# A trunk of Fourier and attention layers: the exact front scales its tables, and the even outputs are added to x outside PSUM

## The chip, the cores and the metric

The kernel runs on one core of one Trainium2 chip. The metric is the device time of one execution in microseconds (us), given as the median of several runs. Five engines matter: TensorE (in profiles PE, with its weight loads as PEld), VectorE (DVE), ScalarE (ACT), GpSimd (POOL) and SyncE (SP). SP, ACT and POOL also issue transfers (DMA), each into its own queue. A transfer issued by POOL can add what it moves to what stands at its destination; such a transfer is called an adding transfer below.

## The reference

Two sequences, `x_prompt` and `x_sample`, each of 512 tokens by 1024 features in float32, pass through the same trunk of two layers. Each layer is a token mixer and an MLP, both behind an RMS norm and both added to x. The mixer of layer 0 is a grouped 2-D Fourier transform, that of layer 1 is attention.

```
def fourier_mix(h, w_out):
    hg = h.reshape(B, S, N_FGROUPS, F_GROUP)          # 8 groups of 128 features
    f = jnp.fft.fft2(hg, axes=(1, 3), norm="ortho").real
    return f.reshape(B, S, D_MODEL) @ w_out

def sq_relu_mlp(h, w_up, w_down):
    a = jnp.maximum(h @ w_up, 0)
    return (a * a) @ w_down

for i in range(2):
    x = x + (fourier_mix if i == 0 else gqa_attention)(rms_norm(x, ...), ...)
    x = x + sq_relu_mlp(rms_norm(x, mlp_norm[i]), mlp_w_up[i], mlp_w_down[i])
return rms_norm(x, final_norm)
```

The change lies in the first 70 us or so, in the Fourier mixer of layer 0 for both sequences. Sequence 0 is `x_prompt`, sequence 1 is `x_sample`.

## The kernel before, in words

**Order.** The whole kernel is written inside `manual_schedule`: each engine executes its instructions in the order in which the program names them, and so do the three queues that issue transfers. A line in the Python text therefore has a place in each engine's list. Waits between engines follow from the data. PSUM has eight banks, handed out by `ps()` in turn, and most tiles in SBUF come from one ring of equal slots, handed out by `slot()`.

**The transform.** The tokens are folded so that a transform of 512 tokens needs two products, a cosine one ("even") and a sine one ("odd"), of half the length; the features of a group are folded in the same way, so that a feature transform is again an even and an odd product. `Front` (L394) prepares a pair of token tiles of 128 tokens: `squares` sums the squares of a tile on ScalarE, `chain` makes the reciprocal root of the norm from them in six small steps (L146 is one of them), `gain` (L410) multiplies by the gains, `plus` and `minus` (L423) fold the features, `plus_there` (L419) does the first of these by an adding transfer inside SBUF, `scale` and `scale_both` (L434, L440) apply the root on ScalarE, and `combine` (L441) folds two token tiles into one by VectorE (L449 for sequence 0, L464 and L465 for sequence 1). For sequence 0 the tiles 0 and 1 aren't folded with each other, so there are three chunks of the token sum in `parts`: tile 0, tile 1, and tiles 2 and 3 together.

**Exact and split products.** Sequence 0 goes first and uses full float32 in its transform, where a product is a pair of matmuls (`exact_even` L504, `exact_odd` L507, and `exact_nyq` L510 for the eight features that the fold leaves over). Its tables come from `exact_table`. Sequence 1, and all products with weights, split each operand into a high and a low half in a faster format, the high half cast by ScalarE (L86) and the low one subtracted by VectorE (L87), and take three matmuls (`mm3`, L81 to L83).

**`transform(q, mid, hook)`** (L578) makes the token products of chunk 0 and 1, calls `mid`, makes those of the last chunk, takes each pair from PSUM (`seq_evac`) and makes four feature stages (`feat_stage`, L541), the results of which go to `uv`. L553 is a product that picks the sums of the odd features, four times per sequence; L552 and L544 are the feature products, L596 and L597 take the left-over rows out of PSUM as `an`. `hook` is called after every stage and puts other work there. Before it, `idle` (L576) issues 39 products of a constant tile, whose result nobody reads.

**The weights** of the mixer come in four pairs, `Fold(0)` to `Fold(3)` (L636): `minus` subtracts on VectorE (L645) and sends an adding transfer of 512 KB from DRAM (L646); `odd` splits the differences, `even_hi` and `even_lo` split the sums (L655, L659). `FoldNyq` does it for the rows left over (L677, L679).

**The outputs.** `odd_outs(0, ...)` makes the odd half of all eight output blocks of sequence 0 in eight PSUM banks. `odd_put` (L720, L721) copies them to x, twice: once as they are and once with the sign turned. `even_outs` then makes the even half, block by block: 12 matmuls of `mm3` and one for the rows left over (L697). `even_put` adds it to both halves of x by VectorE from PSUM (L726), and ScalarE copies the two edge columns (L727). After every second block, `add_input` (L730) sends an adding transfer of 512 KB that brings in the input itself; x is kept as four pairs of blocks, `xs[0, 0]` to `xs[0, 3]`, of 512 KB each. Between these calls stand the steps of the front of sequence 1 (`g0`, `g1`) and the four tables of its transform (`table(k)`, L329, issued by POOL).

**What follows.** SP puts away one pair of sequence 0, loads x of sequence 1 and the first MLP weights. `transform(1)` runs with `hook1`: after its first three token stages ScalarE squares the blocks 0, 1 and 2 of x of sequence 0, after its feature stages the blocks 3 to 7 (`square`, L178), and POOL adds the squares up (L182). Then `even_outs(1)` and `odd_outs(1)` follow, with the MLP of sequence 0 behind them.

## Time and profile before

| | before |
|---|---|
| median of 3 runs | 1672.26 us (1671.59 to 1673.68) |
| the profiled execution | 1673.12 us |
| its span, first to last instruction | 1671.3 us |
| mean granted TensorE clock | 0.999 |
| TensorE busy | 1661.9 us (99%) |
| VectorE busy | 1267.0 us (76%) |
| ScalarE busy | 872.1 us (52%) |
| GpSimd busy | 394.3 us (24%) |
| moved by transfers | 302.48 MB, mean 181 GB/s |

A row of the timeline gives the start of an instruction in us from the span's start, its busy time, the engine, the line of the kernel and the operation, then what it writes and reads by the program's names, and in brackets the idle time of the engine just before it with what ended that. A row ending in x6 stands for six such instructions in sequence. A row of the view of windows gives a stretch, its length, the busy time and number of instructions of each engine (PE, PEld, DVE, ACT, POOL in that order), the granted clock, the busy share of the transfer engines and what they moved in GB/s. In the list of transfers a row ends with the number, the size and the median time from issue to landing.

### The profile page before, as it was taken

The page shows a single profiled execution, that of the slowest core. Times are in us where ns is not written, and L with a number is a line of the kernel's source. Part 1 is how long each engine was busy: PE and PEld are TensorE (multiplying, and loading weights), DVE is VectorE, ACT ScalarE, POOL GpSimd, SP SyncE. Part 2 cuts the span into 40 slices and gives each one's busy share as a digit, 9 for nine tenths or more (in the row PEclk, how much of TensorE's full clock was granted, in tenths as well). Part 3 has the DMA queues.
Part 4 walks back from the last instruction along what each step waited for, and adds up shares of the span by engine and source line. Part 5 has one row for each costly group of instructions (what it writes and reads, how often), then busy time and mean ns, then how long its engine had stood idle before and what let it go on. Part 6 is the DMA issues. An engine that isn't in the chain of part 4 may idle for free.

```text
span 1671.3 us, 22288 instructions
## 1 busy us (share of the span) xinstructions
PE 1661.9 (99%) x7843; PEld 1387.8 (83%) x7843; DVE 1267.0 (76%) x1851; ACT 872.1 (52%) x1540; POOL 394.3 (24%) x364
## 2 busy tenths in 40 slices
PE   9999999999999999999999999999999999999998
PEld 8988887888888888888888888888888888888887
DVE  8879776557886869869888877777855487878875
ACT  7766444446342435447688855554454552433334
POOL 3321444221000001325444303004422220000002
PEclk9999999999999999999999999999999999999999
DMA  9843554449775757425501156334544696757532
GB/s 306 257 158 118 204 195 172 151 170 373 250 228 165 248 170 236 168 77 200 166 1 39 64 176 223 117 120 167 211 145 166 221 375 194 233 158 236 178 104 101
DMA packets 122192, 302.48 MB, mean 181 GB/s; under 512 B 12344, under 2 KB 13496, under 8 KB 122080
## 3 DMA queue, kind: packets, MB, share of 16 engines
q1 hardware_dynamic: 98720, 253.53, 43.9%
q0 software_dynamic: 8960, 21.05, 6.0%
q10 hardware_dynamic: 14400, 26.48, 4.2%
q8 instruction: 61, 1.00, 0.2%
q14 instruction: 51, 0.42, 0.1%
HBM read 217.59 MB, written 82.38 MB: 179 GB/s over the span
## 4 chain that ended last, share of the span: by engine, by line
PE 97%; DVE 1%; DMA 0%; ACT 0%; issue 0%; POOL 0%; DVEq 0%; POOLq 0%; ACTq 0%
PE ps L940 74%; PE ps L83 6%; PE ps L81 6%; PE ps L82 6%; PE ps L1535 2%; PE ps L576 0%; PE ps L1514 0%; DMA raw<-w_up 0%; PE ps L191 0%; PE ps L507 0%; PE ps L504 0%; DVE w L87 0%; DVE raw L990 0%; PE ps L199 0%; DVE raw L989 0%
## 5 line engine op out<-in xcount | busy, mean ns | idle before, releaser
L940 PE MATMUL ps<-u,w 128*128 128x512 f32 x4944 | 1130.9, 389 | 1.2 <-DVE t L1018 1.2
L940 PEld LDWEIGHTS ps<-u,w 128*128 128x128 f32 x4944 | 926.6, 188 | 195.9 <-ACT u L973 1.7
L86 ACT CAST w<-raw 128x1024 fp32r<-128x1024 f32 (+1 forms) x216 | 213.7, 994 | 311.5 <-PE ps L940 234.3
L87 DVE TENSOR_TENSOR w<-raw,w 128x1024 fp32r<-128x1024 f32 (+1 forms) x216 | 252.0, 1170 | 75.7 <-ACT w L86 75.4
L86 ACT CAST u<-u 128x1024 fp32r<-128x1024 f32 x144 | 145.0, 1047 | 85.1 <-PE ps L940 36.4
L87 DVE TENSOR_TENSOR u<-u,u 128x1024 fp32r<-128x1024 f32 x144 | 174.3, 1239 | 17.3 <-ACT u L86 16.0
L940 PE MATMUL ps<-u,u 128*128 128x512 f32 x600 | 143.3, 389 | 0.0
L1150 DVE TENSOR_TENSOR u<-ps,u 128x512 f32<-128x512 f32 x160 | 109.9, 688 | 39.8 <-PE ps L940 37.3
L1177 POOL DMA_DIRECT2D raw<-w_sum x32 | 27.7, 865 | 468.2 <-DMA raw<-w_sum 170.8
L1058 POOL TENSOR_TENSOR u<-u 128x512 f32<-128x512 f32 x28 | 37.0, 1321 | 425.9 <-ACT u L955 425.9
L940 PEld LDWEIGHTS ps<-u,u 128*128 128x128 f32 x600 | 112.5, 188 | 24.1 <-ACT u L973 0.4
L81 PE MATMUL ps<-u,u 128*128 128x512 f32 (+2 forms) x340 | 128.7, 380 | 0.0
L83 PE MATMUL ps<-u,u 128*128 128x512 f32 (+2 forms) x340 | 123.7, 365 | 0.0
L82 PE MATMUL ps<-u,u 128*128 128x512 f32 (+2 forms) x340 | 123.6, 365 | 0.0
L182 POOL TENSOR_TENSOR t<-t,t 128x512 f32<-128x512 f32 (+1 forms) x54 | 79.2, 1470 | 187.0 <-ACT t L178 186.1
L954 ACT ACTIVATE t<-t 128x512 f32<-128x512 f32 x64 | 40.5, 632 | 109.2 <-DVE t L1027 95.7
L83 PEld LDWEIGHTS ps<-u,u 128*128 128x128 f32 x340 | 64.2, 189 | 10.5 <-DVE u L87 0.3
L87 DVE TENSOR_TENSOR u<-ps,u 128x512 fp32r<-128x512 f32 (+3 forms) x112 | 68.2, 636 | 5.6 <-ACT u L86 5.0
L82 PEld LDWEIGHTS ps<-u,u 128*128 128x128 f32 x340 | 64.4, 189 | 8.5 <-DVE u L87 0.3
L81 PEld LDWEIGHTS ps<-u,u 128*128 128x128 f32 x340 | 64.4, 189 | 7.8
L1014 DVE TENSOR_TENSOR t<-ps,u 128x512 f32<-128x512 f32 x32 | 22.0, 689 | 59.5 <-PE ps L940 55.8
L86 ACT CAST u<-ps 128x512 fp32r<-128x512 f32 (+3 forms) x112 | 59.5, 557 | 7.7 <-PE ps L1535 6.1
(270 smaller groups left out, 2024.6 us busy)
## 6 DMA issues: line engine op xcount, KB each, us to landing
raw<-w_up SPq DMA_DIRECT2D x80, 512.0 KB, 4.6
u<-spill_t SPq DMA_DIRECT2D x60, 512.0 KB, 6.7
raw<-w_sum SPq DMA_DIRECT2D x56, 512.0 KB, 5.5
u<-spill_b SPq DMA_DIRECT2D x45, 512.0 KB, 6.3
spill_t<-u SPq DMA_DIRECT2D x84, 256.0 KB, 2.0
spill_b<-t ACTq DMA_DIRECT2D x60, 256.0 KB, 4.4
raw<-w_row SPq DMA_DIRECT2D x28, 512.0 KB, 5.0
park<-u SPq DMA_DIRECT2D x24, 512.0 KB, 4.6
```

Source lines behind the costliest of these rows:

```text
L81: nc.tensor.matmul(out, lh, rh, start=first, stop=False)
L82: nc.tensor.matmul(out, lh, rl, start=False, stop=False)
L83: nc.tensor.matmul(out, ll, rh, start=False, stop=last)
L86: hi = nc.scalar.copy(dst_hi, src)
L87: return hi, eng.tensor_sub(dst_lo, src, f32(dst_hi))
L182: nc.gpsimd.tensor_add(acc[q][:, :n], acc[q][:, :n], s[:, :n])
L940: nc.tensor.matmul(o, w[x][:, sl], h[k][y], start=first and k + i == 0, stop=k == n - 1 and i == 2, skip_group_check=not first)
L954: nc.scalar.activation(t, src, AF.Relu)
L1058: eng.tensor_sub(t[:, 0], b12, b11)
L1150: return nc.vector.tensor_add(x, o, x)
L1177: nc.gpsimd.dma_start(s[:, 1], w[:, 3], accum_op=ALU.add)
L1535: nc.tensor.transpose(pt[:, t * P : (t + 1) * P], probs[t][:, sc * P : (sc + 1) * P], ident)
```

## The change

**The front of sequence 0.** The root of the norm is no longer applied to the folded operands of tiles 0 and 1 but to the rows of the two tables they are multiplied with (`table(i)`, two ScalarE steps in place of six). The tables are laid out anew for it, and each of the tiles 0 and 1 has a root of its own. The inputs and tables are loaded in the order x tile 1, first table, x tile 2, second table, x tile 3; the loads of the four weight pairs follow, with the third table between them, and then x of sequence 1. There are 23 constant products instead of 39 at the start, and nine more, with a zero operand, before `mid`.

**The odd sums of sequence 0.** The four picking products go. VectorE sums the odd features of each chunk (`odd_sums`, three reductions), ScalarE puts the sums beside the left-over features (`put_sums`), and the three products for the left-over features take 56 rows instead of 40 and stand together behind the token products. `put_low` takes the additional rows out. Therefore `transform` is split into `transform_exact(mid, hook)` for sequence 0 and `transform(q, hook)` for sequence 1, and the row positions of the feature table and of `FoldNyq` change from 0, 32, 64 to 8, 16, 40.

**The weights.** All four `minus` stand after the fourth token stage instead of being spread from `mid` to there; the split of the differences follows behind. The loads of x tiles 2 and 3 of sequence 1 wait for one of these splits. The fetch of `FoldNyq` is issued after the transform, with the clearing of two tiles of `Front` and of the edge columns of x; the four tables of sequence 1 are issued before the odd outputs, ahead of the adding transfers of the front. A small product with a mask moves from POOL to VectorE.

**The outputs of sequence 0.** All four folded weights are cast before the first `odd_put`. `add_input` for pairs 0 and 1 is issued after the `odd_put` of their blocks, that for pairs 2 and 3 after the last one, so all four stand before the even outputs. `even_put` is a ScalarE copy from PSUM to a tile of its own, `even_part`, for the pairs 0 and 1 in both halves, for 2 and 3 in one. `add_even` adds it to x: pairs 0 and 1 by one adding transfer of 512 KB each from SBUF to SBUF, issued by POOL behind even output 2 and behind the scaling that follows even output 3; pairs 2 and 3 by VectorE, two instructions each, behind `g1.split_lo()`, the last split ahead of `transform(1)`. `hook1` and what follows are as before.

```diff
         load_x(0, 0, nc.scalar)
         load_x(0, 1)
         exact_table(4)
-        for t in range(2, 4):
-            load_x(0, t)
+        load_x(0, 2)
         exact_table(5)
-        exact_table(6)
+        load_x(0, 3)
...
+    def odd_sums(k):
+        s = small(8)
+        x = parts[k][0].rearrange("p (g d i) -> p g d i", g=8, i=2)[:, :, :, 1]
+        nc.vector.tensor_reduce(s, x, AX.X, ALU.add)
+        return s
+    def put_sums(k, s):
+        nc.scalar.copy(parts[k][2][:, :, 1:], s.unsqueeze(1).unsqueeze(1).broadcast_to([P, 2, 3, 8]))
...
-        def scale_both(self, i):
+        def table(self, i):
+            t = exact[i][:, :514]
+            nc.scalar.activation(t, t, AF.Copy, scale=self.r[:, i : i + 1])
+        def low(self, i):
             if i == 0:
-                self.n = sm.tile([P, 2, 5, 8], F32, tag="ny", name=nm("ny"), bufs=2, padded_shape=[P, 2, 8, 8])
-            for out, x in ((self.p[i], self.p[i]), (self.n[:, i], eights(self.m[i])), (self.m[i], self.m[i])):
-                nc.scalar.activation(out, x, AF.Copy, scale=self.r[:, i : i + 1])
-            parts.append((self.p[i], self.m[i], self.n[:, i]))
+                self.n = nyq_tiles(2)
+            nc.scalar.copy(self.n[i][:, :, 0], eights(self.m[i], 2))
+            parts.append((self.p[i], self.m[i], self.n[i]))
...
+    def idle(o, n, zero=None):
+        w, alone = (filler, True) if zero is None else (zero, False)
         for _ in range(n):
-            nc.tensor.matmul(o[:, :256], filler, filler.unsqueeze(1).broadcast_to([P, 2, P]), start=True, stop=True)
...
+    def put_low(on):
+        norm = 1.0 / math.sqrt(S * P)
+        low = un[0]
+        nc.scalar.activation(low[0:56], on[0:56, :258], AF.Copy, scale=norm)
+        nc.vector.scalar_tensor_tensor(low[32:56], on[32:56, :258], norm, f32(low[32:56]), ALU.mult, ALU.subtract)
...
+    def transform_exact(mid, hook):
+        ov = [(ps(), ps()) for _ in range(4)]
+        for k in range(2):
+            for j in range(4):
+                exact_even(k, j, ov[j][0])
+            for j in range(4):
+                exact_odd(k, j, ov[j][1])
+        idle(ov[3][1], 9, an[:, :P])
+        mid()
+        ab = []
+        for j in range(4):
+            exact_odd(2, j, ov[j][1])
+            exact_even(2, j, ov[j][0])
+            ab.append(seq_evac(0, *ov[j]))
+            hook("seq", j)
+        on = ps()
+        for k in range(3):
+            exact_nyq(k, on)
+        put_an(on)
+        put_low(on)
+        hook("an", 0)
+        o = [feat_exact(*ab[j]) for j in range(2)]
+        for j in range(4):
+            feat_nyq(o[j][0], j)
+            feat_split(0, j, *o[j])
+            hook("feat", j)
+            if 0 < j < 3:
+                o.append(feat_exact(*ab[j + 1]))
...
+        def fetch(self):
+            for r, i in ((8, 0), (16, 1), (40, 0)):
                 nc.gpsimd.dma_start(f32(self.w[r : r + 8]), self.d[i])
...
+    even_part = {}
     def even_put(q, fo, o):
-        x = xt(q, fo)
-        both = x.rearrange("p (h n) -> p h n", h=2)
-        nc.vector.tensor_add(both[:, :, 1:], o[:, 1:256].unsqueeze(1).broadcast_to([P, 2, 255]), both[:, :, 1:])
-        nc.scalar.copy(x[:, 0:257:256], o[:, 0:257:256])
+        i, f = fo // 2, fo % 2
+        if f == 0:
+            even_part[i] = slot([P, 2, 512], F32)
+        nc.scalar.copy(even_part[i][:, f, :257], o[:, :257])
+        if i < 2:
+            nc.scalar.copy(even_part[i][:, f, 257:], o[:, 1:256])
+    def add_even(q, i):
+        x, e = xs[q, i], even_part[i]
+        if i < 2:
+            nc.gpsimd.dma_start(x, e, accum_op=ALU.add)
+            return
+        both = x.rearrange("p f (h n) -> p f h n", h=2)[:, :, :, 1:]
+        nc.vector.tensor_add(both, e[:, :, 1:256].unsqueeze(2).broadcast_to([P, 2, 2, 255]), both)
+        edge = x[:, :, 0:257:256]
+        nc.vector.tensor_add(edge, e[:, :, 0:257:256], edge)
...
-        ftX, pickX = exact[2][:, :256], exact[2][:, 256:334]
+        cosX = [exact[0][:, :258], exact[1][:, :258], exact[0][:, 514:772]]
+        sinX = [exact[0][:, 258:514], exact[1][:, 258:514], exact[1][:, 514:770]]
         f0, f1, wn = Front(0, 0), Front(0, 1), FoldNyq()
+        g0, g1 = [Front(1, c) for c in range(2)]
+        idle(ps(), 23)
+        f0.squares(0)
+        f0.gain(0, 0, halves_gr[0])
+        f0.root(0, 0, 2)
+        nc.scalar.copy(gr[:, :512], halves_gr[0])
+        f0.gain(0, 1, halves_gr[1])
+        nc.scalar.copy(gr[:, 512:], halves_gr[1])
+        f0.root(0, 2, 6)
+        f0.table(0)
+        f0.plus(0)
+        f0.minus(0)
+        f0.squares(1)
         wn.load()
-        idle(ps(), 39)
-        f0.squares(0)
-        for k in range(2):
...
+        fold = [Fold(0)]
+        exact_table(6)
+        fold += [Fold(j) for j in range(1, 4)]
+        for t in range(2):
+            load_x(1, t)
+        nc.sync.dma_start(gc, gcol)
+        f0.gain(1)
+        f0.root(1, 0, 3)
...
+        f0.low(0)
+        f0.low(1)
+        ftX = exact[2][:, :256]
+        f1.gain(0)
         f1.minus(0)
         f1.gain(1)
-        fold = [Fold(j) for j in range(2)]
+        sums3 = []
...
-            fold.append(Fold(2))
-            fold.append(Fold(3))
-            for t in range(NT):
-                load_x(1, t)
-            nc.sync.dma_start(gc, gcol)
-        g0, g1 = [Front(1, c) for c in range(2)]
+            sums3.extend(odd_sums(k) for k in range(3))
...
         def hook0(at, j):
             if at == "seq":
-                if j == 0:
-                    fold[1].minus()
-                    fold[0].odd()
-                elif j == 2:
-                    fold[2].minus()
-                    fold[1].odd()
+                if j == 1:
+                    for k in range(3):
+                        put_sums(k, sums3[k])
                 elif j == 3:
-                    fold[3].minus()
-                    fold[2].odd()
+                    for f in fold:
+                        f.minus()
+                    fold[0].odd_hi()
+            elif at == "an":
+                fold[0].odd_lo()
             elif j == 3:
+                fold[1].odd_hi()
+                low = fold[1].odd_lo()
+                for t in range(2, NT):
+                    behind(load_x(1, t), low, sync=True)
+                fold[2].odd()
                 fold[3].odd()
-                g0.squares(0)
-                g0.gain(0)
-                g0.minus(0)
-                g0.plus_there(0)
-                g0.squares(1)
-                g0.gain(1)
-                g0.minus(1)
-                g0.plus_there(1)
-        transform(0, mid, hook0)
+                for i in range(2):
+                    g0.squares(i)
+                g0.chain(1, 2)
+        transform_exact(mid, hook0)
+        wn.fetch()
+        for x in (g0, g1):
+            x.clear()
         for i in range(4):
             xs[0, i] = slot([P, 2, 512], F32)
+            nc.gpsimd.memset(xs[0, i][:, :, 0:257:256], 0.0)
+        for k in range(4):
+            table(k)
         o = odd_outs(0, range(KC))
-        g0.chain(0, 2)
-        fold[0].even_hi()
-        fold[1].even_hi()
-        g0.chain(2, 6)
+        g0.chain(0, 1)
+        g0.gain(0)
+        g0.chain(2, 3)
+        g0.minus(0)
+        g0.plus_there(0)
+        for j in range(4):
+            fold[j].even_hi()
+        g0.chain(3, 4)
         fold[0].even_lo()
+        g0.chain(4, 5)
         fold[1].even_lo()
+        g0.chain(5, 6)
+        fold[2].even_lo()
+        fold[3].even_lo()
+        for fo in range(2):
+            odd_put(0, fo, o[fo])
+        add_input(0, 0)
         g0.scale(slice(0, 1))
-        fold[2].even_hi()
-        fold[2].even_lo()
-        odd_put(0, 0, o[0])
-        fold[3].even_hi()
-        fold[3].even_lo()
-        for fo in range(1, 4):
+        for fo in range(2, 4):
             odd_put(0, fo, o[fo])
+        add_input(0, 1)
+        g0.gain(1)
+        g0.minus(1)
+        g0.plus_there(1)
         g0.scale(slice(1, 2))
-        g1.gain(0)
+        g1.squares(0)
         for fo in range(4, 6):
             odd_put(0, fo, o[fo])
-        g0.combine()
-        for k in range(4):
-            table(k)
+        g1.gain(0)
+        g1.minus(0)
+        g1.plus_there(0)
+        g1.squares(1)
+        g1.chain(1, 2)
         for fo in range(6, 8):
             odd_put(0, fo, o[fo])
-        g1.minus(0)
-        g1.plus_there(0)
-        g0.split_even()
         g1.gain(1)
-        g0.split_odd()
+        g1.minus(1)
+        g1.plus_there(1)
+        for i in range(2, 4):
+            add_input(0, i)
         def even(fo):
             even_put(0, fo, even_outs(0, [fo])[0])
-            if fo % 2:
-                add_input(0, fo // 2)
-        g1.squares(0)
-        even(0)
-        g1.minus(1)
-        g1.plus_there(1)
-        g1.squares(1)
-        even(1)
-        even(2)
-        g1.chain(0, 2)
+        for fo in range(3):
+            even(fo)
+        g0.combine()
+        g1.chain(0, 1)
+        g1.chain(2, 3)
+        add_even(0, 0)
+        g0.split_even()
+        g1.chain(3, 4)
+        g0.split_odd()
+        g1.chain(4, 6)
         even(3)
-        g1.chain(2, 6)
-        even(4)
         g1.scale(slice(0, 1))
-        even(5)
         g1.scale(slice(1, 2))
-        even(6)
+        add_even(0, 1)
+        for fo in range(4, KC):
+            even(fo)
         g1.combine()
         g1.split_hi()
-        even(7)
         g1.split_lo()
+        for i in range(2, 4):
+            add_even(0, i)
```

More of the change, by code (lines that the diff above doesn't have):

```diff
@@ L399, in __init__ @@
             self.ss, self.r = small(2), small(2)
-            self.steps = rsqrt_steps(self.r[:, :2], self.ss[:, :2], 2, 1.0 / D)
+            if q == 0 and c == 0:
+                self.apart = [rsqrt_steps(self.r[:, i : i + 1], self.ss[:, i : i + 1], 1, 1.0 / D) for i in range(2)]
+            else:
+                self.steps = rsqrt_steps(self.r[:, :2], self.ss[:, :2], 2, 1.0 / D)
             self.xg, self.p, self.m = [None] * 2, [None] * 2, [None] * 2
@@ L741, in trunk_kernel @@
-        idle(ps(), 39)
-        f0.squares(0)
-        for k in range(2):
-            f0.gain(0, k, halves_gr[k])
-            nc.scalar.copy(gr[:, k * 512 : k * 512 + 512], halves_gr[k])
-        f0.minus(0)
-        f0.plus(0)
-        f0.squares(1)
-        f0.gain(1, 0)
-        f0.chain(0, 6)
+        g0, g1 = [Front(1, c) for c in range(2)]
[4 more added lines that the diff above has]
+        nc.scalar.copy(gr[:, :512], halves_gr[0])
@@ L873, in hook1 @@
                     square(0, 7)
[L875 removed]
+        transform(1, hook1)
         for fo in range(KC):
```

175 lines of the change are left out of this document (80 added, 95 removed).

## The prediction

> **What bounds the kernel now.** I read the page's first part, then what TensorE waited for, then the first 90 us by timeline.
>
> ```profile
> span 1671.3 us, 22288 instructions
> PE 1661.9 (99%) x7843; PEld 1387.8 (83%) x7843; DVE 1267.0 (76%) x1851; ACT 872.1 (52%) x1540; POOL 394.3 (24%) x364
> PE ps L576 <- DVE mask L369: 1.2, 1, 1.2
> PE ps L940 <- DVE t L1018: 1.2, 1, 1.2
> PE ps L199 <- DVE s L146: 0.2, 1, 0.2
> PE ps L1535 <- POOL t L1529: 0.2, 1, 0.2
> ```
>
> The last four rows are all that TensorE waited for in the whole span: 2.8 us. So the time is TensorE's list of matmuls, and the change can do two things only: shorten that list, or open waits in it. After the changed stages the list is as dense as before them, so a delay there has nothing behind it that could absorb it. The rows of the list that the change touches (start, time, line, shape):
>
> ```profile
> 5.46 5.75 PE L576 MATMUL ps<-u 128*128 128x256 f32 x39
> 11.05 1.47 PE L504 MATMUL ps<-u,t 128*128 128x258 f32 x6
> 12.45 0.63 PE L510 MATMUL ps<-u,ny 128*40 128x258 f32 x2
> 13.01 1.56 PE L507 MATMUL ps<-u,t 128*128 128x256 f32 x6
> 22.55 1.47 PE L504 MATMUL ps<-u,t 128*128 128x258 f32 x6
> 23.86 1.46 PE L507 MATMUL ps<-u,t 128*128 128x256 f32 x6
> 29.24 0.47 PE L81 MATMUL ps<-u,u 128*128 128x256 f32 x1
> 40.93 0.28 PE L81 MATMUL ps<-u,w 128*128 128x258 f32 x1
> 1.17 2.93 PE L576 MATMUL ps<-u 128*128 128x256 f32 x12 [1.17 <-DVE mask L369]
> 5.30:7.10 1.80, 1.64 (x7) 1.71 (x8) 1.00 1.01 404
> ```
>
> The last row is a window of the fillers (L576) alone: 7 begun by 7.10, so 0.23 us each, and the other 32 in the 3.95 us to 11.05, 0.12 us each. A full-precision product is a pair of matmuls, and three of them take 22.55 to 23.86: 0.435 us each.
>
> The second resource is the transfers. Stages of the first 65 us; the last two columns are the transfer engines' share and GB/s:
>
> ```profile
> 2.50:24.00 21.50, 21.50 (x111) 17.97 (x111) 18.41 (x33) 15.79 (x33) 6.56 (x9) 1.00 1.02 408
> 26.00:39.00 13.00, 13.00 (x97) 12.28 (x96) 12.23 (x22) 10.40 (x20) 3.76 (x6) 1.00 1.07 211
> 39.00:45.50 6.50, 6.50 (x56) 6.50 (x55) 5.95 (x10) 6.50 (x20) 2.45 (x7) 1.00 0.94 266
> 45.50:51.20 5.70, 5.70 (x50) 5.70 (x49) 5.63 (x11) 3.87 (x11) 2.17 (x3) 1.00 0.26 46
> q0 software_dynamic: 864, 2.62, 74.1%
> ```
>
> From 2.5 to 45.5 us they are full. A plain 512 KB (0.524 MB) load costs 1.28 us of them at 408 GB/s. The last row is POOL's queue from 45.5 to 65 us: two adds of 256 KB (L419) and four of 512 KB (L730), 2.62 MB in 74.1% of 19.5 us, 14.45 us; so an adding transfer of 512 KB costs 2.9 us, more than twice a load.
>
> **The change, part by part.** *TensorE's list.* Fillers 39 to 23 and 9 new ones: -7 x 0.12 = -0.84. The four odd-sum products of L553 go: -4 x 0.435 = -1.74. The three narrow products of L510 move together: the one at 12.45 takes 0.56 until 13.01 instead of 0.435, and the three products beside it 1.40 (11.05 to 12.45) instead of 1.31; two such breaks go, about -0.4. Together -3.0 us: that is the most the change can win, 0.18%.
>
> *The front's chain.* With 23 fillers TensorE is free at about 9.2 (11.05 less 16 x 0.12), does 16 products (7.0) and 9 fillers (1.1), and asks for the third chunk at 17.2. VectorE delivers that:
>
> ```profile
> 17.20 0.75 DVE L449 SCALAR_TENSOR_TENSOR t<-t,s,t 128x512 f32<-128x512 f32 x1
> 15.77 0.72 ACT L434 ACTIVATE t<-t,s 128x512 f32<-128x512 f32 x1 [1.59 <-DVE s L146]
> 15.58 0.16 DVE L146 SCALAR_TENSOR_TENSOR s<-s,s 128x2 f32<-128x2 f32 x1
> 20.23 1.23 DVE L645 TENSOR_TENSOR u<-raw,u 128x1024 f32<-128x1024 f32 x1
> ```
>
> It ends at 17.95 now. The new order adds a second root for tile 1 (five steps of 0.16) and saves nothing on VectorE; ScalarE scales a table (0.72) where it scaled two operands (1.44). The tables 4 and 5 arrive by 9 us, as tile 3 now follows table 5. I leave 17.95, +-0.5. TensorE waits 0.7 us, then does 8 products, 3 narrow ones, 8 feature products and 4 small ones: 3.5 + 1.5 + 3.5 + 0.5 = 9.0. The odd outputs start at 26.9 instead of 29.24: -2.3 us. VectorE's three reductions of 256 values (at least 0.31, at most 0.75 each, by the rows for 1024 and 512 columns; I take 0.42) and four subtractions of 1.23 come before the halves of `an`; they end near 24.1 and the half of `an` at 24.5; TensorE wants `an` at 24.7 (17.95 + 8 x 0.435 + 1.5 + 4 x 0.435). That cover is thin: 0.75 for a reduction would be a wait of 1 us.
>
> *Even outputs, start.* Odd outputs last 11.6 (29.24 to 40.93), so TensorE is ready at 38.5. ScalarE now casts all four folded weights before it frees the first PSUM bank. The fourth needs its adding transfer:
>
> ```profile
> 22.70 2.75 POOL L646 DMA_DIRECT2D raw<-w_four  x3
> 31.95 0.86 POOL L646 DMA_DIRECT2D u<-w_four  x1 [6.51 <-issue]
> 36.96 0.85 POOL L419 DMA_DIRECT2D u<-u  x1 [1.56 <-DVE s L146]
> 50.42 2.04 POOL L730 DMA_DIRECT2D u<-xt  x2
> 57.59 0.88 POOL L730 DMA_DIRECT2D u<-xt  x1 [3.03 <-ACT u L596]
> raw<-w_four POOLq DMA_DIRECT2D x1, 512.0 KB, 9.0
> u<-w_four POOLq DMA_DIRECT2D x1, 512.0 KB, 7.2
> u<-xt POOLq DMA_DIRECT2D x1, 512.0 KB, 6.9
> u<-u POOLq DMA_DIRECT2D x1, 256.0 KB, 4.8
> u<-u POOLq DMA_DIRECT2D x1, 256.0 KB, 3.3
> ```
>
> It landed at 31.95 + 7.2 = 39.2. The transfers were full all that while, so only the two loads of x now held back (2.6 us) can bring it forward: 36.6 to 39.2. A cast of 1024 columns and an evacuation later (1.44 and 0.72 at most by the ScalarE row above, 1.6 together is my estimate) the bank is free: 38.2 to 40.8. I take 40.2, as the held loads start near 30 and share. Of the -2.3 us, -0.7 is left. The rows also show POOL stuck: the fourth adding transfer was issued 0.25 us after the first landed (22.70 + 9.0), and the one at 57.59 after 50.42 + 6.9 = 57.3: three are the most outstanding.
>
> *POOL's queue.* In order it now has: four folds, three fetches (32 KB), two memsets and four small ones, four tables, one x add, inputs 0 and 1, three x adds, inputs 2 and 3, even pairs 0 and 1. By 45.5 the old kernel had moved all of it but two x adds and the inputs. So the second x add, 41.8 before (36.96 + 4.8), now lands no sooner than 45.5 + 2 x 2.9 = 51.3. Behind it on VectorE and ScalarE are `combine`, a cast, a row copy and a second cast (up to 0.75 each by the rows for 512 columns, 2.7 to 3.0), two scalings, and the evacuations of even outputs 3 to 7, whose banks the second transform needs: TensorE loses some 2 us there. VectorE then adds pairs 2 and 3 (2 x 1.23) before the second transform's own halves: about 1 us more. These overlap with what follows; they don't add to it.
>
> *The even pairs.* VectorE sheds eight adds and ScalarE gets twelve copies; neither is what decides. The two transfers are: they stand last in POOL's queue. All of it is 14.45 us of work after 45.5, then 2.9 each: pair 0 lands at 62.9, pair 1 at 65.7, if the transfers never pause and nothing else runs. ScalarE needs them in the second transform, whose hook is unchanged: squares 0 and 1 read pair 0, squares 2 and 3 pair 1.
>
> ```profile
> 57.93 0.64 ACT L178 ACTIVATE t<-u 128x512 f32<-128x512 f32 x1
> 60.03 0.67 ACT L178 ACTIVATE t<-u 128x512 f32<-128x512 f32 x1
> 65.03 0.65 ACT L86 CAST u<-ps 128x257 fp32r<-128x257 f32 x2
> 65.42 0.76 DVE L87 TENSOR_TENSOR u<-ps,u 128x257 fp32r<-128x257 f32 x2 [0.32 <-ACT u L86]
> 66.42 0.29 PE L81 MATMUL ps<-u,w 128*128 128x258 f32 x1
> ```
>
> In the old kernel square 0 ran at 57.93 and square 2 at 60.03, each just after its input had landed (57.3 and later). Behind square 2 on ScalarE stand all casts of the second feature stage; TensorE waits for them, through VectorE's halves. From 60.03 to the last half (66.18) are 6.15 us, about 0.65 of it waits for TensorE, so with pair 1 at time L that half is ready at L + 5.5. TensorE wanted it at 66.55 (the matmul behind the 66.42 one). Delay: L - 61.05. At L = 65.7 it is +4.7 us.
>
> Between which L? SP's put-away of pair 2 and four loads of x follow VectorE's add and run beside pair 1. If they begin at 61.8 (an estimate, the second transform's start plus its first stages), 3.9 us of POOL's 20.25 is left; at half the engines it ends at 69.6: +8.6. The row that lies nearest is the first fold, which took 9.0 us to land beside loads of x, where an x add alone took 3.3 us. I take L = 67.3, +6.2 us.
>
> The Trainium skill, "DMA: Bandwidth & Descriptors", Queues, rings and completion order, says that an engine goes round between the queues packet by packet. By that rule an adding packet, being dearer, would get two thirds of the time, and pair 1 would land at 67.7; the 9.0 us of the first fold speak for less than that.
>
> The sum: profiled time 1673.12 + 6.2 = 1679.3; that execution lies 0.86 over the median, so 1678.5.
>
> **Rivals.** *A, the other side: pairs arrive in time.* If pair 1 lands before about 60 us, no square waits, and the front's gain stays less its small waits: -0.5 to -2.9 us, 1669.4 to 1671.8. For it: 4.2 us of the transfers lay idle from 45.5 to 51.2 (26% share). Against it: the new work (5.8) is more than that. It decides at L below 61.
> *B, pairs half late:* L 61 to 64.4, if moves inside SBUF are cheaper than 2.9: 1672.3 to 1675.6. Against: the same 256 KB adds have been measured inside SBUF at that price.
> *C, TensorE slows after its wait.* Fillers at first took 0.23 us and ran so until 7.1. If a wait of 3 us brings that back for as long as it lasted (1.17 to 7.1), half of 5.9 us is lost on top: 1681.4. Against: the clock column stands at 1.00 in every row, no wait of that size is in the trace. The Trainium skill, "TensorE: Matmul & The Clock Gate", Part 1, states just this: an idle window of about 3.4 us halves the clock until one busy window has passed; by its figure 1.7 us, an estimate of 1680.2. The trace's slow start agrees with it in kind, not in length.
> *D, nothing moves:* the gain of the front and the loss behind it cancel by chance; contained in B.
>
> **How the numbers follow.** Main case (1675.7 to 1681) 0.56, C or worse 0.08, B 0.15, A 0.21, of it 0.03 under -0.2%, which a front chain earlier than 17.95 and an uncounted wait would need. 0.2%, 3.3 us, is about what a measurement of this kernel tells from no change. Slower 0.64, same 0.33, faster 0.03. The range leaves out a little on both sides: 1670.2 to 1681.5; the likeliest alone 1675.7 to 1681.
>
> **What would show it.** Right: odd outputs starting near 27; the second x add landing after 50; square 2 on ScalarE idle for some us, released by a transfer; TensorE's first waits of over 1 us between 52 and 72; the second even outputs some 6 us later. Wrong: pair 1 landed before 62, or the transfers idle between 45 and 60. Then a cheaper adding transfer, or a queue not in order, is my error.

## The result, and the profile after

The changed kernel takes 1677.46 us (median of 8 runs, 1675.79 to 1679.1), the kernel before 1672.71 us (8 runs). The ratio is 1.0026 with a 95% interval of 1.0015 to 1.0037: slower by 4.75 us, a little over a quarter per cent. Forecast were 1678.5 us and a range of 1670.2 to 1681.5. The profiled execution took 1676.81 us.

First part of the page after, and the first six rows of what TensorE waited for (in total, times, longest):

```profile
span 1675.0 us, 22279 instructions
PE 1662.4 (99%) x7828; PEld 1386.3 (83%) x7828; DVE 1264.7 (76%) x1855; ACT 872.8 (52%) x1546; POOL 391.5 (23%) x370
PE ps L604 <- DVE mask L368: 1.2, 1, 1.2
PE ps L81 <- ACT u L777: 1.1, 1, 1.1
PE ps L532 <- DVE t L471: 1.0, 1, 1.0
PE ps L82 <- DVE u L87: 0.9, 1, 0.9
PE ps L1029 <- DVE t L1239: 0.5, 1, 0.5
PE ps L81 <- ACT u L769: 0.4, 1, 0.4
```

Before, there were four waits, 2.8 us in all, and none between the start and 260 us but the 0.2 us at L199. After, the wait at the start (L604) is the same, and four of the other five shown lie in the changed stages. Line numbers have moved: L769 and L777 are ScalarE's copies of odd and of even outputs, L471 is `combine`. TensorE by timeline:

```profile
17.99 0.70 PE L532 MATMUL ps<-u,t 128*128 128x256 f32 x2 [0.98 <-DVE t L471]
27.38 0.34 PE L81 MATMUL ps<-u,u 128*128 128x256 f32 x1
46.01 0.39 PE L81 MATMUL ps<-u,w 128*128 128x258 f32 x1 [0.39 <-ACT u L769]
55.61 0.39 PE L81 MATMUL ps<-u,u 128*128 128x256 f32 x1 [1.14 <-ACT u L777]
61.72 0.39 PE L82 MATMUL ps<-u,u 128*128 128x258 f32 x1 [0.89 <-DVE u L87]
70.72 0.39 PE L745 MATMUL ps<-u,u 72*128 72x258 f32 x1
```

The odd outputs start at 27.38, 1.86 us earlier than before. The last row is the final matmul of the first even block of sequence 1. Before, it stood here:

```profile
66.79 0.29 PE L697 MATMUL ps<-u,u 72*128 72x258 f32 x1
```

So TensorE goes from 1.86 us ahead to 3.93 us behind within 43 us. I use this row as the marker below. A marker belongs to the one profiled execution of a kernel; it tells the difference of the medians to within 0.1 to 1.8 us (table below). The transfers behind it (POOL's issues, then landings of those issued at 36.44, 43.95, 52.90 and 56.42), and who waits for them:

```profile
36.44 0.90 POOL L438 DMA_DIRECT2D u<-u  x1 [2.18 <-DVE w L705]
43.95 0.88 POOL L438 DMA_DIRECT2D u<-u  x1 [1.00 <-issue]
52.90 0.87 POOL L784 DMA_DIRECT2D u<-u  x1 [0.38 <-issue]
56.42 0.86 POOL L784 DMA_DIRECT2D u<-u  x1 [2.65 <-ACT u L777]
u<-u POOLq DMA_DIRECT2D x1, 256.0 KB, 7.2
u<-u POOLq DMA_DIRECT2D x1, 256.0 KB, 6.1
u<-u POOLq DMA_DIRECT2D x1, 512.0 KB, 9.0
u<-u POOLq DMA_DIRECT2D x1, 512.0 KB, 8.3
43.66 0.72 ACT L453 ACTIVATE u<-u,s 128x512 f32<-128x512 f32 x1 [3.60 <-DMA u<-u]
50.12 0.75 DVE L485 SCALAR_TENSOR_TENSOR u<-u,s,u 128x512 f32<-128x512 f32 x1 [4.09 <-ACT u L779]
58.26 1.21 DVE L787 TENSOR_TENSOR u<-u,u 128x1020 f32<-128x1020 f32 x1
60.78 0.42 DVE L608 TENSOR_TENSOR u<-ps,u 8x258 fp32r<-8x258 f32 x1
61.95 0.63 ACT L178 ACTIVATE t<-u 128x512 f32<-128x512 f32 x1 [2.76 <-DMA u<-u]
64.78 0.63 ACT L178 ACTIVATE t<-u 128x512 f32<-128x512 f32 x1 [0.59 <-DMA u<-u]
```

Pair 0 lands at 61.9 (52.90 + 9.0), pair 1 at 64.7 (56.42 + 8.3), and ScalarE's squares 0 and 2 start at just those times, having waited 2.76 and 0.59 us. For pair 1's issue at 56.42 the profile names the copy L777 as the releaser, but the copies it needed had ended by 53.5. What ended at 56.1 is the input issued at 50.32, which left two of 512 KB in flight: as in the kernel before, POOL did not have more than three of that size out at once. Two more delays belong here. The front's first adding transfer takes 7.2 us, and ScalarE stands for 3.60 us before `scale`. Its second lands at 50.05 (43.95 + 6.1), and VectorE starts `combine` at 50.12 after 4.09 us of idling. The profile names ScalarE's L779 as the releaser, which ends at just that time; in e_squares, e_order and e_all_vec it names the transfer for the same wait, of 4.4 to 4.7 us. VectorE then comes to its first half of the second transform (L608) at 60.78; before, it was there at 57.11.

The spans of the two profiled executions differ by 3.7 us, nearly the marker's 3.93, but that is a net figure. The execution of before lost 1.66 us at one place, with the slow matmuls behind this wait:

```profile
260.25 0.96 PE L940 MATMUL ps<-u,w 128*128 128x512 f32 x3 [1.15 <-DVE t L1018]
```

It is in the profile of no other kernel, whether 1.6 us ahead or 17 us behind at that place, so I take it for a chance of that one execution. The changed kernel's lost some 1.2 us between 959 and 1532 us, 0.5 of it in the wait at L1029. The medians are 4.75 us apart; the 0.8 us beyond the marker are not placed.

### The profile page after: what moved, and what is told of

Same layout as the page of the kernel before. It is cut to its first block, busy times and chain, and to the rows that moved or that the text cites. A ratio compares the mean times of both kernels' runs of the same rounds, so it can differ in the third digit from the quotient of the medians.

```text
span 1675.0 us, 22279 instructions
## 1 busy us (share of the span) xinstructions
PE 1662.4 (99%) x7828; PEld 1386.3 (83%) x7828; DVE 1264.7 (76%) x1855; ACT 872.8 (52%) x1546; POOL 391.5 (23%) x370
## 4 chain that ended last, share of the span: by engine, by line
PE 94%; DVE 2%; DMA 2%; ACT 1%; issue 0%; POOL 0%; SPq 0%; DVEq 0%; ACTq 0%; POOLq 0%
PE ps L1029 74%; PE ps L83 6%; PE ps L82 6%; PE ps L81 6%; PE ps L1624 2%; DMA u<-u 1%; DMA u<-spill_b 1%; PE ps L1603 0%; PE ps L191 0%; ACT u L86 0%; DVE u L429 0%; DMA u<-spill_t 0%; ACT w L702 0%; DVE u L87 0%; DVE t L442 0%
## 5 line engine op out<-in xcount | busy, mean ns | idle before, releaser
L1029 PE MATMUL ps<-u,w 128*128 128x512 f32 x4944 | 1131.0, 389 | 0.0
L1029 PEld LDWEIGHTS ps<-u,w 128*128 128x128 f32 x4944 | 926.4, 188 | 195.0 <-ACT u L1062 1.7
L86 ACT CAST u<-u 128x1024 fp32r<-128x1024 f32 (+1 forms) x140 | 140.7, 1046 | 85.3 <-PE ps L1029 37.9
L87 DVE TENSOR_TENSOR u<-u,u 128x1024 fp32r<-128x1024 f32 (+1 forms) x140 | 168.7, 1232 | 19.6 <-ACT u L86 19.1
L1029 PE MATMUL ps<-u,u 128*128 128x512 f32 x600 | 143.4, 389 | 0.5 <-DVE t L1239 0.5
L1029 PEld LDWEIGHTS ps<-u,u 128*128 128x128 f32 x600 | 112.5, 188 | 24.6 <-DVE t L1239 0.9
L178 ACT ACTIVATE t<-u 128x512 f32<-128x512 f32 (+1 forms) x64 | 38.1, 606 | 48.4 <-DVE u L1836 20.9
```

Of the source, the lines that this page charges most:

```text
L86: hi = nc.scalar.copy(dst_hi, src)
L87: return hi, eng.tensor_sub(dst_lo, src, f32(dst_hi))
L178: made = nc.scalar.activation(s[:, :n], xt(q, fo)[:, :n], AF.Square)
L1029: nc.tensor.matmul(o, w[x][:, sl], h[k][y], start=first and k + i == 0, stop=k == n - 1 and i == 2, skip_group_check=not first)
```

## The experiments

Each kernel is the changed one with the edit shown; each comparison is with runs of the kernel before on the same chip. Ratios are to it, and the marker is the row at 66.79 us of before. The profiled execution of e_adds is the slowest of its five runs, 2.9 us above their median.

| kernel | time us (before) | ratio, 95% interval | marker against before |
|---|---|---|---|
| the change | 1677.46 (1672.71) | 1.0026 (1.0015 to 1.0037) | +3.93 |
| e_squares | 1675.51 (1672.34) | 1.0015 (1.0006 to 1.0024) | +2.90 |
| e_adds | 1679.78 (1672.34) | 1.0041 (1.0026 to 1.0055) | +9.27 |
| e_all_vec | 1675.65 (1672.34) | 1.0018 (1.0009 to 1.0027) | +3.14 |
| e_old_even | 1673.35 (1672.34) | 1.0005 (0.9996 to 1.0014) | +1.15 |
| e_order | 1675.76 (1672.41) | 1.0018 (1.0009 to 1.0026) | +3.20 |
| e_tables | 1679.50 (1672.41) | 1.0044 (1.0031 to 1.0057) | +8.50 |
| e_best | 1678.78 (1672.41) | 1.0039 (1.0026 to 1.0053) | +5.26 |
| e_double | 1689.70 (1672.41) | 1.0104 (1.0090 to 1.0118) | +16.79 |
| e_old_tables | 1672.82 (1672.71) | 0.9999 (0.9990 to 1.0008) | +0.30 |
| e_mix1 | 1674.12 (1672.71) | 1.0007 (0.9998 to 1.0016) | +1.94 |
| e_mix2 | 1674.19 (1672.71) | 1.0008 (0.9999 to 1.0017) | +2.31 |
| e_fewer_adds | 1670.89 (1672.38) | 0.9993 (0.9983 to 1.0002) | -1.58 |

**e_squares: the reader of the late pairs goes last.**

```diff
-                if j < 3: square(0, j)
-            else: square(0, 3 + j)          # and 7 at the end
+            late = (4, 5, 6, 7, 0, 1, 2, 3)
+                if j < 3: square(0, late[j], first=4)
+            else: square(0, late[3 + j], first=4)
```

> The squares of the second transform in the order 4 to 7, then 0 to 3; transfers and VectorE untouched. Theory (late pair transfers hold ScalarE, and ScalarE holds TensorE): ScalarE's waits of 2.76 and 0.59 us for a transfer go, and the time falls by 1.5 to 3 us against the changed kernel, to 1674.5 to 1676. Rival (VectorE's two adds of 1.37 us ahead of its halves are the bound): the last halves come no earlier, 1677 to 1678.

ScalarE's waits for transfers in the second transform are gone, and the time is about 1.6 us less than the change's (+3.17 against +4.75 over the runs of before beside each). The two intervals overlap, and the markers are 1.0 us apart, so 1.6 us is a rough size. Some 3 us of loss remain without the pairs' lateness.

**e_order: the pairs are made early.**

```diff
-        for i in range(2, 4): add_input(0, i)      # ahead of the even outputs
...
         for i in range(2, 4):
             add_even(0, i)
+            add_input(0, i)
```

> The inputs of pairs 2 and 3 go behind the adding transfers of pairs 0 and 1 in POOL's queue (and behind VectorE's adds of pairs 2 and 3). Same work, other order. Theory (pairs 0 and 1 are late because they stand last in the queue): they land some 5 us earlier, near 57 and 60, ScalarE's wait of 2.76 us for a transfer goes, and the time falls to that of the kernel with the squares in another order, 1675 to 1676; VectorE's adds still stand before its halves. Rival (it is not their place in the queue): 1677 to 1678.

Pair 0 now lands at 56.1 (issued at 51.45, 4.6 us), no early square waits, and the time is that of e_squares. Two ways of taking the same wait away, one at the writer and one at the reader, give the same 3.2 to 3.4 us over before. That two ways agree carries more than either time alone: the wait was one of two delays that lie side by side.

**e_adds: VectorE's adds of pairs 2 and 3 go behind token stages 1 and 2 of the second transform.**

```diff
-        for i in range(2, 4): add_even(0, i)       # ahead of transform(1)
...
                 if j < 3: square(0, j)
+                if 0 < j < 3: add_even(0, 1 + j)
...                                            # put_away, load_xs and the first MLP weights move there too
```

> VectorE's adds of pairs 2 and 3 go behind the second and third token stage of the second transform, with the loads of x that wait for pair 2. Theory (late pair transfers): ScalarE still waits for pair 0 until about 62 and for pair 1 until about 64.8, so 1677 to 1678.5. Rival (VectorE's adds): TensorE's wait at 61.7 goes and the time falls by 1.5 to 2.5 us, to 1675 to 1676.

Neither theory foresaw 1679.8: ScalarE still waited 2.87 us for pair 0, as the theory said, but the adds then stood in front of the later halves, and TensorE waited three more times for VectorE, 4.5 us in all. The profiled execution also ran at half its TensorE clock for 3.4 us behind these waits (last section). The run tells nothing on the rival; it shows that the 2.5 us of adds have no gap in that stage.

**e_all_vec: no pair by transfer.**

```diff
     def add_even(q, i):
-        if i < 2:
-            nc.gpsimd.dma_start(x, e, accum_op=ALU.add)
-            return
```

> Pairs 0 and 1 are added by VectorE too, at the place where the transfers were issued; two adding transfers fewer. Theory (late pair transfers): no ScalarE wait for a transfer in the second transform; VectorE's 2.7 us more are half absorbed by its idle time there; 1674 to 1677. Rival (VectorE's adds are the bound): 2.7 us more of them, 1678.5 to 1680.5.

1675.65, within the theory's range. But something not foreseen is in it, shown in the last section: TensorE ran at half its clock for 3.4 us.

**e_old_even: the new front, the old even outputs.**

```diff
+        nc.vector.tensor_add(both[:, :, 1:], o[:, 1:256]..., both[:, :, 1:])   # even_put, from PSUM
+        nc.scalar.copy(x[:, 0:257:256], o[:, 0:257:256])
...
+            if fo % 2: add_input(0, fo // 2)       # none ahead of the even outputs; no add_even
```

> The new front and odd sums with the even outputs of the kernel before (VectorE adds from PSUM, the input added by transfer after every second block). Theory (the whole loss lies in the even outputs): the shorter list of matmuls shows, 1669.5 to 1671.5, below the kernel before. Rival (the new front itself costs, by its transfers and ScalarE's wait at 43.7 us): 1674 or more.

Neither: 1673.35. The even outputs carry most of the loss (1677.46 to 1673.35, 3.7 us over the runs beside each), but the shorter list of matmuls does not show. TensorE starts the odd outputs 1.3 us earlier than before and is 1.15 us late at the marker.

**e_tables and e_best: the other place in POOL's queue.**

```diff
-        for k in range(4): table(k)                # ahead of the odd outputs
...
         g0.plus_there(1)
+        for k in range(4): table(k)
```

> The four tables of sequence 1 are issued behind the second adding transfer of the front instead of ahead of the first. Theory (the first such transfer lands at 43.6 us since 1.45 MB of tables are moved with it, and holds ScalarE for 3.6 us): it lands near 40, that wait shrinks to under 1 us, TensorE's wait of 0.4 us at 46.0 goes; the pairs land as late as before, so the time falls by less than 1 us, 1676.5 to 1677.5. Rival (the transfer is slow by itself or POOL issues it late): ScalarE's wait stays above 2.5 us.

The first adding transfer landed after 3.8 instead of 7.2 us and ScalarE's early wait went, as expected. The forecast of the time failed, by how much the pairs moved: what the tables no longer delay they delay later.

```profile
65.85 0.63 ACT L178 ACTIVATE t<-u 128x512 f32<-128x512 f32 x1 [4.61 <-DMA u<-u]
69.35 0.63 ACT L178 ACTIVATE t<-u 128x512 f32<-128x512 f32 x1 [1.26 <-DMA u<-u]
```

Pair 0 lands 3.9 us later than in the changed kernel, pair 1 4.6 us; the span is 3.7 us longer. VectorE waits for transfers as well and comes to its first half (L608) 3.8 us later, and TensorE runs at half its clock twice (last section): the run delays both paths. e_best combined this with e_order and put all four adding transfers of the front ahead of inputs 0 and 1.

> Both orders together: all four adding transfers of the front first, with the tables behind the second; then inputs 0 and 1, pairs 0 and 1, and last inputs 2 and 3. Theory (both queue places cost, and VectorE's list ahead of the second transform is the next bound): VectorE's wait of 4.1 us at 50.1 shrinks, its halves start about 2 us earlier than in the changed kernel, 1672 to 1674.5. Rival (only the pairs' place costs): as with the inputs of pairs 2 and 3 moved alone, 1675 to 1676.

Neither: 1678.78. VectorE's wait of 4.1 us at 50 us went, but it waited 3.26 us for the front's last adding transfer, and the transfer engines had little to do from 39 to 45.5 us (share 0.30, against 1.12 in the changed kernel); pair 0 landed at 62.2 again, and ScalarE waited 4.13 us for it.

```profile
54.47 0.75 DVE L485 SCALAR_TENSOR_TENSOR u<-u,s,u 128x512 f32<-128x512 f32 x1 [3.26 <-DMA u<-u]
59.72 0.42 DVE L608 TENSOR_TENSOR u<-ps,u 8x258 fp32r<-8x258 f32 x1
66.11 0.63 ACT L178 ACTIVATE t<-u 128x512 f32<-128x512 f32 x1 [1.64 <-DMA u<-u]
```

Of all the runs this one parts the two paths best. VectorE is at its first half 1.06 us earlier than in the changed kernel (59.72 against 60.78), square 2 starts 1.33 us later (66.11 against 64.78), and the marker is 1.33 us later. The time goes with the pairs.

**e_double: one more adding transfer in front of the pairs.**

```diff
         for i in range(2, 4): add_input(0, i)
+        add_input(0, 3)
```

> One adding transfer of 512 KB more ahead of those of pairs 0 and 1: the input of pair 3 is added twice, which changes the output. Theory (the landing of the pairs sets the time, at 2.9 us of the transfer engines for 512 KB): they land 2.5 to 2.9 us later, near 64.7 and 67.5, and the time is 1679.5 to 1681. Rival (VectorE's adds set it and the transfers only nearly): ScalarE's wait grows and the time stays below 1678.5.

The delay is far larger than 2.9 us. The second add to the same tile was not issued before the first had landed, and POOL's whole queue stood:

```profile
60.57 0.87 POOL L792 DMA_DIRECT2D u<-xt  x1 [7.58 <-DMA u<-xt]
69.93 1.22 DVE L787 TENSOR_TENSOR u<-u,u 128x1020 f32<-128x1020 f32 x1 [9.94 <-DMA u<-xt]
73.77 0.63 ACT L178 ACTIVATE t<-u 128x512 f32<-128x512 f32 x1 [14.14 <-DMA u<-u]
77.65 0.63 ACT L178 ACTIVATE t<-u 128x512 f32<-128x512 f32 x1 [1.65 <-DMA u<-u]
```

As a test of a doubled price it failed. Pair 0 is there at 73.77 instead of 61.95, 11.8 us later, and the span is 12.6 us longer (1687.6 against 1675.0). But VectorE's add of pair 3 also waited, 9.94 us for the doubled input, so this run too delays both paths, and TensorE ran at half its clock for 10.2 us of it. With e_tables it agrees with a time that follows the pairs' landing about one for one; by themselves the two do not show it.

**e_old_tables, e_fewer_adds: where the front's gain goes.** Both go on from e_old_even. The first has the tables behind the first adding transfer.

```diff
         g0.plus_there(0)
+        for k in range(4): table(k)                # no longer ahead of the odd outputs
```

> The new front with the old even outputs, and the four tables issued behind the first adding transfer of the front instead of ahead of it. Theory (with the late pairs gone, what eats the shorter list is VectorE's list, held up through ScalarE by the first adding transfer, which lands late behind the tables): ScalarE's wait of 3.8 us at 44 us shrinks below 1.5 us, VectorE starts the second transform's halves 0.5 to 1.3 us earlier than 58.4, and the time is 1671.8 to 1672.8, 0.5 to 1.5 us below the kernel with the old even outputs alone. Rival (TensorE is bound by something else there): 1673.3.

ScalarE's wait shrank to 1.20 us, VectorE came to the second transform at 57.52, and the marker stands 0.85 us earlier than in e_old_even. The time, 1672.82, equals before (0.9990 to 1.0008). The bound shows in a window of the end of the even outputs (busy time of PE, PEld, DVE, ACT, POOL), first before, then e_old_tables:

```profile
51.20:58.00 6.80, 6.80 (x59) 6.78 (x59) 6.29 (x15) 3.98 (x13) 2.71 (x5) 1.00 1.02 177
```

```profile
51.20:58.00 6.80, 5.72 (x44) 4.97 (x43) 6.70 (x16) 3.94 (x13) 2.58 (x3) 1.00 0.76 130
```

TensorE had no gap there before; now it has 1.08 us, and VectorE is full. So I took work from VectorE alone, by leaving the adds of the first four blocks out of x:

```diff
+        if fo > 3:
             nc.vector.tensor_add(both[:, :, 1:], o[:, 1:256]..., both[:, :, 1:])
```

> The kernel with the new front, the old even outputs and the tables behind the first adding transfer, without VectorE's adds for the first four even output blocks, which leaves these out of x: 2.5 us of VectorE's list ahead of the second transform go, nothing of TensorE's. Theory (VectorE's list there is what hides the shorter list of matmuls): TensorE's waits for the token halves at 53.8 and 56.3 us go, it is 1.2 to 1.9 us earlier at 80 us than with them, and the time is 1671 to 1671.8. Rival (TensorE is bound there by transfers or ScalarE): the waits stay, 1672.5 to 1673.

```profile
51.20:58.00 6.80, 6.80 (x57) 6.66 (x57) 6.37 (x14) 5.07 (x16) 1.73 (x2) 1.00 1.03 195
```

Both waits are gone, TensorE is full, the marker is 1.88 us earlier than in e_old_tables, and the time is 1670.89. By median and marker the shorter list is worth 1.5 to 1.6 us against the kernel before, though the interval (0.9983 to 1.0002) still touches 1, and only to a VectorE with 2.5 us less to do.

**e_mix1, e_mix2: can a pair go by transfer for nothing?** From e_old_tables, with pair 0, or pairs 0 and 1, by transfer ahead of the later inputs, and VectorE adding the other pairs from PSUM.

```diff
+            if fo % 2 and fo < 2: add_even(0, fo // 2)     # fo < 4 in e_mix2
+            elif fo % 2: add_input(0, fo // 2)
```

> As that, but pair 0 by an adding transfer that stands behind the front's four and ahead of inputs 1 to 3; input 0 stands where the change put it; VectorE adds pairs 1 to 3 from PSUM. VectorE sheds 1.25 us. Theory (an adding transfer is free where its landing has room: near 55 us here, wanted at 58): no ScalarE wait for a transfer in the second transform, and 1670.8 to 1672.3. Rival (any adding transfer more delays the others, for the transfer engines are full): ScalarE or VectorE wait for one of the front's, 1673 or more.

> Pairs 0 and 1 both by adding transfers behind the front's four, ahead of inputs 2 and 3; inputs 0 and 1 ahead of the front's last two; VectorE adds pairs 2 and 3 from PSUM. Theory: VectorE sheds 2.5 us, pair 1 lands near 58 to 60, where it is wanted at 60; 1670 to 1673, with the front's last transfers, 3 us later, as the risk. Rival (queue full): 1674 or more.

The rivals held. No square waited, yet the two were 1.3 and 1.4 us slower than e_old_tables. In e_mix1 VectorE waited 2.85 us for the front's second adding transfer, in e_mix2 4.47 us. Input 0 now stands ahead of that one in the queue, as it does in the change. No version of mine with the whole computation beat the kernel before.

## Why the prediction was right, and where it was not

**Direction, size and place** held: forecast +6.2 us, measured +4.75. Square 2 on ScalarE waits for a transfer, and the even outputs of sequence 1 come 3.9 us late. The direction and the range alone would have held without the pairs, too: e_squares and e_order, in which no square waits for them, are slower than before by 3.2 to 3.4 us. That the mechanism was right is seen from the markers. In the four kernels in which square 2 waits for pair 1 (the change, e_best, e_tables, e_double), the marker is the start of square 2 (64.78, 66.11, 69.35, 77.65) less 60.85, within 0.01 us; the prediction had its landing less 61.05.

**The landing of the pairs** is the term that was mis-sized. I put pair 1 at 65.7 at the least and took 67.3; it landed at 64.7. My formula, landing less 61.05, gives 3.7 for that, and the marker says 3.93. Three things stand behind that. The price held: from 45.5 us to the landing at 64.7, POOL's queue moved 3.27 MB in 92.2% of 19.2 us, 5.4 us per MB, against 5.5 in the row of the prediction (2.62 MB in 14.45 us). The bound failed because it let the new kernel have moved by 45.5 us just what the old had: POOL's queue had moved 4.68 MB by then, and 4.27 before, since three folds are issued earlier (0.54 MB instead of 0.13 from 15 to 26 us). And the 1.6 us added for sharing did not come: SP issued its put-away at 59.62, but until 62.9 POOL's queue still filled the transfer engines (95% of their time from 62.4 on). The rows of the transfer engines for the stages between:

```profile
26.00:39.00 13.00, 13.00 (x104) 12.61 (x103) 12.68 (x24) 12.63 (x25) 5.89 (x15) 1.00 1.06 278
39.00:45.50 6.50, 6.50 (x56) 6.42 (x54) 6.40 (x8) 2.90 (x8) 2.60 (x3) 1.00 1.12 245
45.50:51.20 5.70, 5.31 (x45) 5.19 (x44) 1.61 (x5) 5.48 (x19) 2.57 (x3) 1.00 0.98 182
```

The 278 GB/s of the first row, against 211 before, are mostly plain loads that now fall there (1.03 MB instead of 0.30). The share column says that transfers did not pause: 4.2 us that lay idle before (26% from 45.5 to 51.2) are in use, and it isn't enough.

**The front's chain**: odd outputs at 26.9 forecast, 27.38 measured. The third chunk was delivered at 17.93 as I left it, TensorE waited 0.98 instead of 0.7 us, and the stage behind it took 9.4 instead of 9.0 us. The reductions took 1.07 us for three:

```profile
18.51 1.07 DVE L400 TENSOR_REDUCE s<-t 128x8 f32<-128x256 f32 x3
```

**The start of the even outputs**: I left 0.7 us of the gain, 1.72 were left (40.67 against 42.39 for the end of the first block). The fourth fold was issued at 28.16 and landed at 35.7, below my range of 36.6 to 39.2, since I had not let POOL issue it earlier.

**The step that failed** is in the paragraph on POOL's queue: that the second adding transfer of the front (51.3 forecast, 50.05 measured) and VectorE's adds of pairs 2 and 3 "overlap with what follows; they don't add to it". True for the sum, which goes by the later of two paths. But that paragraph itself put some 3 us on the other path, and rival A left them out as "small waits": pairs in time would not have given 1669.4 to 1671.8 but 1675.5 to 1675.8. e_squares and e_order show that the other path alone is worth about 3 us on this side of the front's gain. So rival A held a price far too low. And the first paragraph's "the time is TensorE's list" overlooked that VectorE had been nearly as full as TensorE in the same stretch (12.23 of 13.00 us from 26 to 39 before, 12.68 after): e_old_tables and e_fewer_adds show that the list of matmuls could not be shortened by itself.

**What is shown and what is argued.** Shown: the pairs' lateness sets the time of the changed kernel; taken away at the writer or the reader, it gives back 1.4 to 1.6 us by the medians and 0.7 to 1.0 by the markers. What is left then goes with VectorE: in e_squares, e_order and e_all_vec the marker is the time of VectorE's first half (61.33, 61.66, 61.57) less 58.45, and in the five kernels in which VectorE adds from PSUM (e_old_even and those made from it) that time less 57.2, each within 0.03 us. In the changed kernel VectorE comes at 60.78, by the first of these a marker of +2.3; as an estimate from these rows the pairs cost the other 1.6 us. Shown also: with the old even outputs the marker moves ahead when VectorE has less to do, and the time with it, so far as its interval tells. Argued from rows alone: that VectorE is late in the change by the wait for the second adding transfer and by the adds of pairs 2 and 3, and in what parts. The two weren't told apart: e_adds tried and could not.

## What to carry to other kernels

Where a trace shows TensorE without gaps, look at which other engine is as full in the same stretch; shortening one list moves the bound to the other, here for a gain of nothing. Work taken off an engine and given to a queue that runs in order costs by its place in that queue: list what stands ahead of it, add up the transfer engines' time for it, and compare the landing with the first reader. And when one late arrival is taken away, ask what is late next before counting the gain.

## What the hardware showed that I had not expected

The granted clock falls though TensorE is not idle. In e_all_vec (busy time of PE, clock, share of transfers, GB/s):

```profile
53.00:56.40 3.40, 1.71 (x10) 0.99 0.98 177
56.40:59.60 3.20, 3.19 (x15) 0.50 0.61 118
```

In this run the clock stood at 0.50 from 56.31 to 59.72 us, for 3.41 us, and 15 matmuls took 0.21 us each instead of 0.12: some 1.4 us of TensorE's work. What of it the time felt is open, since VectorE came from its adds to its first half without a gap. The clock fell in the same way in e_adds, e_tables and e_double, so their times contain such stretches too, and in no other run between its first and its last microseconds. Counting back from each fall in steps of 3.41 us gives the work of TensorE in the step just before a fall, and the two emptiest steps at full clock in these runs that no fall followed:

| run | step, us | TensorE's work in it, us | clock in the next step |
|---|---|---|---|
| e_double | 62.63 to 66.04 | 0.00 | 0.50 |
| e_tables | 63.03 to 66.44 | 0.94 | 0.50 |
| e_adds | 68.99 to 72.40 | 1.20 | 0.50 |
| e_tables | 52.79 to 56.20 | 1.32 | 0.50 |
| e_all_vec | 52.90 to 56.31 | 1.81 | 0.50 |
| e_double | 59.22 to 62.63 | 2.02 | 1.00 |
| e_adds | 62.16 to 65.57 | 2.06 | 1.00 |

So in these runs the clock fell after a step with 1.81 us of work or less and stayed after one with 2.02 us or more. In the changed kernel it stayed at 1.00, with 2.04 us of work from 53.00 to 56.40. Rival C's slowing is real, then, but the changed kernel stayed clear of it. The Trainium skill, "TensorE: Matmul & The Clock Gate", Part 1, speaks of an idle window of 3.4 us; the length of the penalty, 3.41 us, agrees with this trace, but here a step did not have to be idle: 1.81 us of work in it were not enough to keep the clock.

VectorE was slow ahead of the chance wait of before at 260 us:

```profile
251.25 1.82 DVE L989 TENSOR_TENSOR raw<-raw,raw 128x512 f32<-128x512 f32 x1 [2.99 <-DMA raw<-w_up]
255.23 1.77 DVE L990 TENSOR_TENSOR raw<-raw 128x512 f32<-128x512 f32 x1
```

GpSimd worked on tiles of its own from 251.2 to 258 us. Of the 64 instructions of these two lines in the trace of before, the 35 beside which GpSimd computed nothing took 0.68 to 0.70 us; the other 29 took up to 1.82. So the slowness goes with GpSimd's work. That the one causes the other is argued from the times; no run tested it.
